# A hybrid trunk layer on one core: one PSUM pool, blocks kept in SBUF at a hand-over, a staggered output pass, and earlier weight loads

## The chip, the cores and the metric

The kernel runs on one core of a Trainium2 chip, as one program. The metric is the device time of one execution in microseconds; lower is better. A core has five engines that run their own instruction queues: TensorE (PE in the profile; its weight loads are PEld), VectorE (DVE), ScalarE (ACT), GpSimd (POOL) and SyncE (SP), which issues nearly all transfers here. TensorE writes to PSUM, which has eight banks of 128 x 512 float32.

## The reference

One layer over 2048 tokens of width 1024, all in float32:

```
h  = rmsnorm(x) ; proj = h @ w_in                        # 1024 -> 5648 columns
y_a = u_b * conv3(u_c * u_h)                             # short convolution mixer, 1024 wide
y_b = rmsnorm_grouped(ssd_scan(silu(conv4(xbc)), dt) * silu(z))   # Mamba-2 mixer, 1024 wide
x  = x + concat(y_a, y_b) @ w_out                        # 2048 -> 1024
x  = x + square(relu(rmsnorm(x) @ w_up)) @ w_down        # 1024 -> 4096 -> 1024
out = rmsnorm(x)
```

## The kernel before

**Arithmetic.** Every float32 operand is split into a rounded high part and a remainder (`hi`, `lo`: a cast on ScalarE, a subtraction on VectorE), and a product is three matmuls, hi x hi, hi x lo and lo x hi. The large projections use the seven-product scheme of Strassen and Winograd on 2 x 2 blocks: tokens in two blocks of 512, contraction in halves, two column tiles of 128. The seven operands of the token side are called b11, t1, t2, b21, t3, b22, t4. They lie in `places`: place 0 holds b11 and t1, place 1 t2 and b21, place 2 t3 and b22, place 3 t4, each four times, for k = 0 to 3, as tiles uh and ul of four buffers per place.

**Stages.** The input projection runs in two halves of 1024 tokens (`first_half`, 20 pairs of column tiles; `second_half`, 22). The scan's first half runs beside the second. `Output` then does the output projection in four passes of 16 units; a unit is one block of 512 tokens times one tile of 128 output columns, 24 matmuls into one PSUM bank, an addition of the residual on VectorE (L1452) and a store. Pass 0 and 1 take the contraction's first half, pass 2 and 3 the second; passes 0 and 2 take token blocks 0 and 1, passes 1 and 3 blocks 2 and 3. In a pass the two blocks alternate for every column tile d. The scan's second half runs beside units 0 to 44. The MLP follows in two halves of 16 pairs, then the down projection and its rest.

**A pair.** `chain` runs the seven products, 12 matmuls each, with accumulators x, y (PSUM tag mm) and w (tag mw); w is seeded with a copy of x after b11, except in the first two pairs of the MLP (`fresh`). After each product come the eviction, then work on the next pair's weights, then `after(name)`. The generator `ahead` first issues the next pair's loads (`next(ahead)`, into `wraw`, three buffers) after the product t1; its four splits are taken after b21 (two), b22 and t4. In the later halves the sums of weights come back from DRAM (`sums_d`), with three loads at the start and a fourth in between.

**Preparation of the other half.** `prepare` is a generator of 32 steps (22 where the sums of squares are there already). It loads two token blocks, sums squares, forms the inverse root, loads the blocks again (tiles nb), scales them (L393), subtracts them into the seven operands (L208) and stores those in DRAM (`stored`: hm_d or hn_d). `after` takes one step at each product. At the last pair of a half, `refresh` fetches the operands of the next half place by place (tiles rb; `fetch`) and splits them (`settle`, L344 and L345).

**The hand-over.** For the MLP's first half, `prepare(0, ...)` runs during the last output pass: `hook` is called twice in a unit, at half of it and at its end, and takes one or two steps. The operands go to hn_d and are fetched again: place 2 at call 19 of the pass, place 3 at 22, place 0 at 28 and place 1 at 31, each settled when it has come and its uh and ul buffers are free; block 2's operands of the output projection occupy the buffers of place 0, block 3's those of place 1. The MLP's first weights are loaded before unit 62; two splits are taken there, one before unit 63, one after it.

**PSUM.** The pool `ps` (tag tp, two banks) lives throughout. Pool `pa` has six banks up to the end of the output projection (mm three, mw one, yo and yd of the scan one each); it is closed, and `pw` opened in its place (mm four, mw two).

**Order.** The source calls the engines in the order described, but each engine's instruction order is made by the compiler from the dependences and its own estimate; neighbours can change places. Each engine then takes its queue in order.

Of the kernel before, what the change touches and what calls it, by code (L numbers as in the profile page):

```python
# [11 lines left out]
F32 = mybir.dt.float32  # L12
# [27 lines left out]
def trunk(ctx: ExitStack, tc: tile.TileContext, x, w_in, w_dt, w_out, w_up, w_down, cvec, hrow, out):  # L40
# [9 lines left out]
    accs = {}  # L50

    edge = ctx.enter_context(tc.tile_pool(name="edge", bufs=1, side="right")).tile([P, 24], F32, name="edge")
    nc.gpsimd.memset(edge, 0.0)
# [61 lines left out]
        nc.tensor.matmul(out, wlo, hi, start=False, stop=(k == nk - 1))  # L115

    def psum(tag, name, bufs=1):
        pool = ps if tag == "tp" else accs["pool"]
        return pool.tile([P, 512], F32, tag=tag, name=name, bufs=bufs)

    class Rstd:

# [67 lines left out]
    class Seven:  # L190
# [53 lines left out]
        def chain(self, groups, ws, ahead, evict, after):  # L244

            n = sum(len(g) for g in groups)
            pm = [{} for _ in groups]
            got = []
            seeds = self.seeds = set()
            bank = lambda acc: psum(*(("mw", "pw", accs["mw"]) if acc == "w" else ("mm", "p" + acc, accs["mm"])))  # L250
            fresh = max(accs.get("fresh", 0), 0)
            accs["fresh"] = fresh - len(groups)
            PRODUCTS = (
                ("b11", 0, 0, "x"),
                ("t1", 1, 0, "y"),
                ("t2", 1, 1, "x"),
                ("b21", 0, 1, "w"),
                ("t3", 2, 0, "x"),
                ("b22", 2, 1, "y"),
                ("t4", 3, 0, "x"),  # L260
            )
            for name, wn, half, acc in PRODUCTS:
                at = half * n
                for gi, g in enumerate(groups):
                    seeded = acc in pm[gi]
                    if not seeded:
                        pm[gi][acc] = bank(acc)
                    p = pm[gi][acc]
                    i, j = WHERE[name]
                    for k, place in enumerate(g):  # L270
                        hi, lo = (t[:, (at + k) * P : (at + k + 1) * P] for t in ws[wn])
                        h = [t[:, j] for t in place[i]]
                        kw = dict(skip_group_check=seeded)
                        nc.tensor.matmul(p, hi, h[0], start=not seeded and k == 0, stop=False, **kw)  # L274
                        nc.tensor.matmul(p, hi, h[1], start=False, stop=False, **kw)  # L275
                        nc.tensor.matmul(p, lo, h[0], start=False, stop=(k == len(g) - 1), **kw)  # L276
                    at += len(g)
                for gi in range(len(groups)):
                    if name == "b11" and gi >= fresh:
                        pm[gi]["w"] = bank("w")  # L280
                        nc.scalar.copy(pm[gi]["w"], pm[gi]["x"])  # L281
                        seeds.add(gi)
                    evict(name, gi, pm[gi])
                if ahead is not None:
                    if name == "t1":
                        next(ahead)
                    got += take(ahead, {"b21": 2, "b22": 1, "t4": 1}.get(name, 0))
                after(name)
            return got
# [51 lines left out]
        def settle(self, places, i, got):  # L341
            for p, t in zip(places, got):
                p[i] = self.place(i)
                nc.scalar.copy(p[i][0], t)  # L344
                nc.vector.tensor_tensor(out=p[i][1], in0=t, in1=p[i][0].bitcast(F32), op=ALU.subtract)  # L345

# [8 lines left out]
        def prepare(self, h, src, base, accs=None):  # L355
# [26 lines left out]
                st.whole(rs[bb])  # L382
                yield
            for k in range(4):
                ts = [self.raw("nb") for _ in range(4)]
                b11, t1, t2, b21, t3, b22, t4, b12 = (t[:, i] for t in ts for i in range(2))
                blocks = ((b11, 0, k), (b12, 1, k), (b22, 1, 4 + k), (b21, 0, 4 + k))
                for o, bb, f in blocks:
                    nc.sync.dma_start(o, src[h * NBB + bb][:, f])
                yield  # L390
                yield
                for o, bb, f in blocks:
                    nc.vector.scalar_tensor_tensor(  # L393
                        out=o, in0=o, scalar=col(base, f), in1=rs[bb], op0=ALU.mult, op1=ALU.mult
                    )
# [5 lines left out]
                for i in range(3):  # L401
                    nc.sync.dma_start(self.stored[h][k][:, 2 * i : 2 * i + 2], ts[i])
                nc.sync.dma_start(self.stored[h][k][:, 6], t4)
                yield

        def facc(self):
            return self.up.tile([P, TB], F32, tag="facc", name="facc", bufs=2)
# [10 lines left out]
    class Proj(Seven):  # L418
# [105 lines left out]

        def group(self, bb, ws, tiles, work, tag="mm"):

            pm = [psum(tag, "pm", accs[tag]) for _ in tiles]
# [255 lines left out]
        def first_half(self, ws):  # L783
            self.last_sums()
            late = self.prepare(1, x, C_NMIX)
            for m, what in enumerate(self.PAIRS):
# [7 lines left out]
                    ahead = self.weights(0, self.PAIRS[m + 1])  # L794

                def after(name):
                    next(late, None)
                    if last:
                        self.refresh(name)

# [21 lines left out]

    class Mlp(Seven):
        stored = hn_d

        def tmp(self, name):
            return self.up.tile([P, TB], F32, tag="utmp", name=name, bufs=8)
# [61 lines left out]
        def half(self, h, ws, late):  # L889
            for q in range(NQ):  # L890
# [10 lines left out]
                    self.new = [{} for _ in range(4)]  # L901

                def after(name):
                    next(late, None)
                    if not last:
                        return
                    if h == 0:
# [125 lines left out]
        def rest(self, ws):  # L1033
# [12 lines left out]
            for bb, t0, w in ((0, 0, TB), (1, 0, TB // 2), (1, TB // 2, TB // 2)):  # L1046
# [13 lines left out]
                for (d, fs, blocks), (whi, wlo) in ws:  # L1060
                    for i in range(2):
# [1 line left out]
                        if not at:  # L1063
                            continue
                        step()
                        pm = psum("mm", "pm", 4)[:, 0:w]
# [90 lines left out]
    class Scan:  # L1157
# [96 lines left out]
        def back(self, n):  # L1254
# [6 lines left out]
            yo = psum("yo", "yo")  # L1261
# [4 lines left out]
            yd = psum("yd", "yd")  # L1266
# [25 lines left out]
            pss = psum("tp", "pss", 2) if self.bufs == 1 else psum("mw", "pss", accs["mw"])  # L1292
# [73 lines left out]
    class Output:  # L1366
# [1 line left out]


        PASSES = [(0, ((0, 0), (1, 1))), (0, ((2, 2), (3, 0))), (1, ((0, 1), (1, 2))), (1, ((2, 0), (3, 1)))]  # L1370
        UNITS = [(i, b, d) for i, bs in PASSES for d in range(KD) for b, _ in bs]
        WEIGHTS = [(i, d) for i, _ in PASSES for d in range(KD)]

        def __init__(self, places):
# [64 lines left out]
        def unit(self, n, hook):  # L1439

            i, b, d = self.UNITS[n]
            self.residual(n + 1)
            if n % 2 == 0:
                self.weights(n // 2 + 2)
            pm = psum("mm", "pm", accs["mm"])
            whi, wlo = self.ws[n // 2]
            for k in range(KD):
                if k == KD // 2:
                    hook(2 * n)
# [8 lines left out]
        def square(self, b, d, t):  # L1458
# [2 lines left out]
                self.accs.append(self.xp.tile([P, TB], F32, tag="facc", name="facc", bufs=2))  # L1461
                nc.scalar.activation(self.accs[b], t, AF.Square)
            else:
                sq = psum("mw", "sq", accs["mw"])
# [21 lines left out]
            put(1, 3, 1, 90, (94, 94, 95, 95))  # L1486


    accs.update(mm=3, mw=1)
    c4 = ctx.enter_context(ExitStack())  # L1490
    with ExitStack() as c1:
        accs["pool"] = c1.enter_context(tc.tile_pool(name="pa", bufs=1, space=PS, reuse_waits="tile"))
        proj = Proj()
        with ExitStack() as c2:
            proj.open(c2, 0)
# [33 lines left out]
        mlp.raws = c4.enter_context(tc.tile_pool(name="ur", bufs=1, side="right", reuse_waits="tile"))  # L1529
        mlp.up = proj_out.xp  # L1530
        mlp.us = c4.enter_context(tc.tile_pool(name="us", bufs=1, side="right", reuse_waits="tile"))
        late = mlp.prepare(0, x1_d, C_NMLP, proj_out.accs)
# [90 lines left out]
```

## Time and profile before

| what | value |
|---|---|
| median of 3 runs | 2684.56 us (2682.47 to 2686.77) |
| profiled execution, its own time | 2686.92 us |
| its span, first to last instruction | 2685.2 us |
| TensorE, VectorE, ScalarE, GpSimd busy | 2608.8, 1876.7, 1431.9, 147.9 us |
| mean granted TensorE clock | 0.992 of full |
| moved by DMA | 551.64 MB, mean 205 GB/s |

Times in the profile count from the first instruction. A timeline row gives the start, the duration, the engine, the source line, the operation and its tiles; in brackets stands the idle time of the engine just before it and what ended that. A row of a view by stretches gives the stretch, its length, the busy time and number of instructions of PE, PEld, DVE, ACT and POOL, then the granted clock, the share of the DMA engines' time and GB/s. A row of grouped instructions ends in busy us, mean ns of one, and the idle time before them. A row of transfers ends in their number, the size of one and the us from issue to landing. SPq, ACTq and the like are the engines' issuing queues. Matmuls are pipelined: the duration in a row overlaps the next, and the distance of starts is what counts.

### The profile page before, as it was taken

The page shows a single profiled execution, that of the slowest core. Times are in us where ns is not written, and L with a number is a line of the kernel's source. Part 1 is how long each engine was busy: PE and PEld are TensorE (multiplying, and loading weights), DVE is VectorE, ACT ScalarE, POOL GpSimd, SP SyncE. Part 2 cuts the span into 40 slices and gives each one's busy share as a digit, 9 for nine tenths or more (in the row PEclk, how much of TensorE's full clock was granted, in tenths as well). Part 3 has the DMA queues.
Part 4 walks back from the last instruction along what each step waited for, and adds up shares of the span by engine and source line. Part 5 has one row for each costly group of instructions (what it writes and reads, how often), then busy time and mean ns, then how long its engine had stood idle before and what let it go on. Part 6 is the DMA issues. An engine that isn't in the chain of part 4 may idle for free. (4 is left out here: it accounts for less than half of the span.)

```text
span 2685.2 us, 33606 instructions
## 1 busy us (share of the span) xinstructions
PE 2608.8 (97%) x12024; PEld 2126.4 (79%) x12024; DVE 1876.7 (70%) x2524; ACT 1431.9 (53%) x2176; POOL 147.9 (6%) x162
## 2 busy tenths in 40 slices
PE   7999999999999999998989999999999999999998
PEld 5778888788887888776877788888887888888887
DVE  7996667667667676666668655644447877888985
ACT  6644345766667676666326455655555444444443
POOL 0010000111111101111000000000000000000001
PEclk9999999999999999999999999999999999999999
DMA  3585345645545588876598875765558545665762
GB/s 144 194 312 185 130 141 203 183 152 180 178 153 171 161 278 259 252 209 210 196 311 292 328 255 192 253 238 203 184 207 276 168 152 152 199 223 169 243 207 74
DMA packets 297479, 551.64 MB, mean 205 GB/s; under 512 B 26720, under 2 KB 142432, under 8 KB 297312
## 3 DMA queue, kind: packets, MB, share of 16 engines
q1 hardware_dynamic: 297312, 549.50, 61.6%
q8 instruction: 94, 1.54, 0.2%
q14 instruction: 73, 0.60, 0.1%
HBM read 362.23 MB, written 187.17 MB: 205 GB/s over the span
## 5 line engine op out<-in xcount | busy, mean ns | idle before, releaser
L274 PE MATMUL px<-uh,whi 128*128 128x512 f32 x1672 | 660.3, 395 | 23.3 <-DVE xt L1452 7.7
L276 PE MATMUL px<-uh,wlo 128*128 128x512 f32 x1672 | 653.7, 391 | 2.2 <-DVE wlo L101 2.2
L275 PE MATMUL px<-ul,whi 128*128 128x512 f32 x1672 | 654.2, 391 | 0.6 <-DVE ul L345 0.5
L274 PEld LDWEIGHTS px<-uh,whi 128*128 128x128 f32 x1672 | 315.4, 189 | 101.1 <-issue 9.5
L101 DVE TENSOR_TENSOR wlo<-wraw,whi 128x1024 fp32r<-128x1024 f32 x214 | 223.7, 1045 | 227.5 <-ACT whi L100 221.7
L276 PEld LDWEIGHTS px<-uh,wlo 128*128 128x128 f32 x1672 | 315.4, 189 | 70.4 <-DVE wlo L101 3.8
L275 PEld LDWEIGHTS px<-ul,whi 128*128 128x128 f32 x1672 | 315.7, 189 | 65.5 <-DVE ul L345 1.8
L100 ACT CAST whi<-wraw 128x1024 fp32r<-128x1024 f32 x214 | 193.5, 905 | 316.1 <-PE px L275 205.6
L274 PE MATMUL py<-uh,whi 128*128 128x512 f32 x836 | 327.8, 392 | 4.7 <-DVE acc L994 3.5
L100 ACT CAST whi<-s 128x1024 fp32r<-128x1024 f32 x210 | 219.4, 1046 | 210.5 <-PE py L275 74.1
L275 PE MATMUL py<-ul,whi 128*128 128x512 f32 x836 | 326.1, 390 | 0.0
L276 PE MATMUL py<-uh,wlo 128*128 128x512 f32 x836 | 325.9, 390 | 0.0
L101 DVE TENSOR_TENSOR wlo<-s,whi 128x1024 fp32r<-128x1024 f32 x210 | 255.3, 1217 | 72.6 <-ACT whi L100 69.6
L113 PE MATMUL pm<-uh,whi 128*128 128x512 f32 (+1 forms) x648 | 252.2, 390 | 2.1 <-ACT uh L204 2.1
L114 PE MATMUL pm<-ul,whi 128*128 128x512 f32 (+1 forms) x648 | 249.3, 385 | 0.0
L115 PE MATMUL pm<-uh,wlo 128*128 128x512 f32 (+1 forms) x648 | 249.0, 384 | 0.0
L274 PEld LDWEIGHTS py<-uh,whi 128*128 128x128 f32 x836 | 157.5, 188 | 39.3 <-DVE acc L994 3.9
L276 PEld LDWEIGHTS py<-uh,wlo 128*128 128x128 f32 x836 | 157.2, 188 | 33.1 <-DVE wlo L101 0.2
L275 PEld LDWEIGHTS py<-ul,whi 128*128 128x128 f32 x836 | 157.3, 188 | 32.2
L274 PE MATMUL pw<-uh,whi 128*128 128x512 f32 x418 | 163.6, 391 | 1.4 <-ACT pw L281 1.4
L276 PE MATMUL pw<-uh,wlo 128*128 128x512 f32 x418 | 162.7, 389 | 0.0
L275 PE MATMUL pw<-ul,whi 128*128 128x512 f32 x418 | 162.7, 389 | 0.0
(220 smaller groups left out, 3719.0 us busy)
## 6 DMA issues: line engine op xcount, KB each, us to landing
hid_d<-e SPq DMA_DIRECT2D x96, 512.0 KB, 4.2
rh<-hid_d SPq DMA_DIRECT2D x96, 512.0 KB, 4.4
wraw<-w_in SPq DMA_DIRECT2D x68, 512.0 KB, 3.9
wraw<-w_down SPq DMA_DIRECT2D x104, 256.0 KB, 3.7
wraw<-w_up SPq DMA_DIRECT2D x48, 512.0 KB, 4.7
dec<-rd_d SPq DMA_DIRECT2D x32, 512.0 KB, 5.5
wraw<-w_out SPq DMA_DIRECT2D x32, 512.0 KB, 5.6
x_d<-xt SPq DMA_DIRECT2D x64, 256.0 KB, 3.7
```

What stands on the lines that cost most here:

```text
L100: nc.scalar.copy(hi, raw)
L101: eng.tensor_tensor(out=lo, in0=raw, in1=hi.bitcast(F32), op=ALU.subtract)
L113: nc.tensor.matmul(out, whi, hi, start=(k == 0), stop=False)
L114: nc.tensor.matmul(out, whi, lo, start=False, stop=False)
L115: nc.tensor.matmul(out, wlo, hi, start=False, stop=(k == nk - 1))
L274: nc.tensor.matmul(p, hi, h[0], start=not seeded and k == 0, stop=False, **kw)
L275: nc.tensor.matmul(p, hi, h[1], start=False, stop=False, **kw)
L276: nc.tensor.matmul(p, lo, h[0], start=False, stop=(k == len(g) - 1), **kw)
```

## The change

1. `psum` knows one pool. Six banks are tags k0 to k5. Up to the end of the output projection mm goes round k0, k1, k2 and mw is k3, with k4 and k5 for the scan's yo and yd; after it mm goes round k0, k1, k2, k4 and mw round k3, k5.
2. In `chain` the next pair's loads are issued after b11, not after t1.
3. `after` takes a step of the preparation at two products of seven in `first_half`, at three of seven in the MLP's first half.
4. The last output pass runs block 3 one column tile behind block 2 (its units: block 2 tile 0, block 2 tile 1, block 3 tile 0, block 2 tile 2, ...), so that block 2 ends with unit 61.
5. For the MLP's first half nothing goes to hn_d. The tiles of place 0 lie in the output projection's ry buffers, those of place 1 in a new pool `stay` (three buffers; the fourth is a raw buffer); those of places 2 and 3 are split at once, in `stow`. Place 0 is settled at the end of unit 61, place 1 after unit 63.
6. `hook` takes one step at each call. The MLP's first weights are loaded before unit 60, with a split before each of the units 61, 62 and 63 and one after.

```diff
+    turns = {"mm": itertools.cycle(("k0", "k1", "k2")), "mw": itertools.cycle(("k3",))}
     def psum(tag, name, bufs=1):
-        pool = ps if tag == "tp" else accs["pool"]
-        return pool.tile([P, 512], F32, tag=tag, name=name, bufs=bufs)
+        if tag in turns:
+            tag = next(turns[tag])
+        return ps.tile([P, 512], F32, tag=tag, name=name, bufs=bufs)
...
                 if ahead is not None:
-                    if name == "t1":
+                    if name == "b11":
                         next(ahead)
...
         def settle(self, places, i, got):
             for p, t in zip(places, got):
                 p[i] = self.place(i)
+                t = t[:, 0:1] if i == 3 else t
...
-                ts = [self.raw("nb") for _ in range(4)]
+                ts = self.blocks(h, k)
...
+                self.stow(h, k, ts)
+                yield
+
+        def stow(self, h, k, ts):
+            for i in range(3):
+                nc.sync.dma_start(self.stored[h][k][:, 2 * i : 2 * i + 2], ts[i])
+            nc.sync.dma_start(self.stored[h][k][:, 6], ts[3][:, 0])
...
 (first_half)
                 def after(name):
-                    next(late, None)
+                    if name in ("b11", "b21"):
+                        next(late, None)
...
 (Mlp)
+        def blocks(self, h, k):
+            if h:
+                return super().blocks(h, k)
+            return [self.early(), self.stay(k), self.raw("nb"), self.raw("nb")]
+
+        def stow(self, h, k, ts):
+            if h:
+                return super().stow(h, k, ts)
+            self.held.append(ts[0:2])
+            for i in (2, 3):
+                self.settle(self.places[k : k + 1], i, ts[i : i + 1])
...
                 def after(name):
-                    next(late, None)
+                    if name in ("b11", "t2", "t3"):
+                        next(late, None)
...
 (Output)
-        UNITS = [(i, b, d) for i, bs in PASSES for d in range(KD) for b, _ in bs]
+        UNITS = [(i, b, d) for i, bs in PASSES[:3] for d in range(KD) for b, _ in bs]
+        UNITS += [(1, b, d - b + 2) for d in range(KD + 1) for b in (2, 3) if 0 <= d - b + 2 < KD]
...
+        mlp.held = []
+        mlp.early = lambda: proj_out.raw("first")
+        mlp.stay = lambda k: mlp.raw("nb") if k == 3 else stay.tile([P, 2, TB], F32, tag="stay", name="stay", bufs=3)
         late = mlp.prepare(0, x1_d, C_NMLP, proj_out.accs)
 
-        held = {}
-        fetches, settles = {19: 2, 22: 3, 28: 0, 31: 1}, {21: 2, 24: 3, 30: 0}
-
         def hook(at):
-            u = at - 2 * 48
-            for _ in range(1 + (u % 3 == 0)):
-                next(late, None)
-            if u in settles:
-                i = settles[u]
-                mlp.settle(mlp.places, i, held[i])
-            if u in fetches:
-                i = fetches[u]
-                held[i] = mlp.fetch(0, i)
+            next(late, None)
+            if at == 2 * 61 + 1:
+                mlp.settle(mlp.places, 0, [t[0] for t in mlp.held])
 
         for n in range(48, 64):
-            if n == 62:
+            if n == 60:
                 ahead = mlp.sums_of(0, 0)
                 next(ahead)
-                ws = take(ahead, 2)
-            elif n == 63:
-                ws += take(ahead, 1)
+            elif n > 60:
+                ws = take(ahead, 1) if n == 61 else ws + take(ahead, 1)
             proj_out.unit(n, hook)
+        mlp.settle(mlp.places, 1, [t[1] for t in mlp.held])
         ws += take(ahead)
-        mlp.settle(mlp.places, 1, held[1])
-    accs.update(mm=4, mw=2, fresh=2, pool=c4.enter_context(tc.tile_pool(name="pw", bufs=1, space=PS, reuse_waits="tile")))
+        c7.close()
+    turns.update(mm=itertools.cycle(("k0", "k1", "k2", "k4")), mw=itertools.cycle(("k3", "k5")), fresh=("k3", "k5"))
```

More of the change, by code (lines that the diff above doesn't have):

```diff
@@ L249, in chain @@
             seeds = self.seeds = set()
-            bank = lambda acc: psum(*(("mw", "pw", accs["mw"]) if acc == "w" else ("mm", "p" + acc, accs["mm"])))
-            fresh = max(accs.get("fresh", 0), 0)
-            accs["fresh"] = fresh - len(groups)
+            bank = lambda acc: psum("mw" if acc == "w" else "mm", "p" + acc)
+            fresh = turns.pop("fresh", ())
+            if fresh:
+                turns["fresh"] = fresh[1:]
             PRODUCTS = (
@@ L278, in chain @@
                 for gi in range(len(groups)):
-                    if name == "b11" and gi >= fresh:
+                    if name == "b11" and not fresh:
                         pm[gi]["w"] = bank("w")
@@ L400, in prepare @@
                 self.sub(t4, b21, t2)
-                for i in range(3):
-                    nc.sync.dma_start(self.stored[h][k][:, 2 * i : 2 * i + 2], ts[i])
-                nc.sync.dma_start(self.stored[h][k][:, 6], t4)
+                self.stow(h, k, ts)
                 yield
+        def blocks(self, h, k):
+            return [self.raw("nb") for _ in range(4)]
+        def stow(self, h, k, ts):
+            for i in range(3):
+                nc.sync.dma_start(self.stored[h][k][:, 2 * i : 2 * i + 2], ts[i])
+            nc.sync.dma_start(self.stored[h][k][:, 6], ts[3][:, 0])
         def facc(self):
@@ L525, in group @@
         def group(self, bb, ws, tiles, work, tag="mm"):
-            pm = [psum(tag, "pm", accs[tag]) for _ in tiles]
+            pm = [psum(tag, "pm") for _ in tiles]
             for k in range(KD):
@@ L824, in trunk, with blocks @@
         stored = hn_d
+        stay = None
+        def blocks(self, h, k):
+            if h:
[7 more added lines that the diff above has]
+                self.settle(self.places[k : k + 1], i, ts[i : i + 1])
         def tmp(self, name):
@@ L1065, in rest @@
                         step()
-                        pm = psum("mm", "pm", 4)[:, 0:w]
+                        pm = psum("mm", "pm")[:, 0:w]
                         todo = [(b * len(fs) + k, j, f) for b, j in at for k, f in enumerate(fs)]
@@ L1260, in back @@
             state = self.state[g]
-            yo = psum("yo", "yo")
+            yo = psum("k4", "yo")
             for j in range(4):
@@ L1265, in back @@
             nc.tensor.matmul(st, t["btok"], t["xde"], start=True, stop=True)
-            yd = psum("yd", "yd")
+            yd = psum("k5", "yd")
             for i in range(HG):
@@ L1291, in back @@
             yield
-            pss = psum("tp", "pss", 2) if self.bufs == 1 else psum("mw", "pss", accs["mw"])
+            pss = psum("tp", "pss", 2) if self.bufs == 1 else psum("mw", "pss")
             nc.tensor.matmul(pss[:, 0:L], ones, ssq, start=True, stop=True)
@@ L1442, in unit @@
             self.residual(n + 1)
[L1443 to L1446, printed above, removed]
+            m = (2 * i + b // 2) * KD + d
+            if b % 2 == 0:
+                self.weights(m + 2)
+            pm = psum("mm", "pm")
+            whi, wlo = self.ws[m]
             for k in range(KD):
@@ L1463, in square @@
             else:
-                sq = psum("mw", "sq", accs["mw"])
+                sq = psum("mw", "sq")
                 nc.scalar.activation(sq, t, AF.Square)
@@ L1486, in schedule @@
             put(1, 3, 1, 90, (94, 94, 95, 95))
-    accs.update(mm=3, mw=1)
     c4 = ctx.enter_context(ExitStack())
     with ExitStack() as c1:
-        accs["pool"] = c1.enter_context(tc.tile_pool(name="pa", bufs=1, space=PS, reuse_waits="tile"))
         proj = Proj()
```

3 lines of the change are left out of this document (2 added, 1 removed).

## The prediction

> **What bounds the kernel now.** I read the page's totals first, then the busy time in stretches of 50 us, then every wait of TensorE in order of time, and for the long waits the queues of VectorE, ScalarE and SyncE around them. The totals say that TensorE is the bound nearly everywhere:
>
> ```profile
> PE 2608.8 (97%) x12024; PEld 2126.4 (79%) x12024; DVE 1876.7 (70%) x2524; ACT 1431.9 (53%) x2176; POOL 147.9 (6%) x162
> ```
>
> So a gain can only come from the stretches where TensorE is not full. By stretch (TensorE busy and matmuls first; then weight loads, DVE, ACT, POOL; granted clock, DMA share, GB/s):
>
> ```profile
> 150.00:200.00 50.00, 47.12 (x204) 37.53 (x202) 49.20 (x64) 23.68 (x29) 7.63 (x9) 1.00 0.86 320
> 1350.00:1400.00 50.00, 50.00 (x222) 41.42 (x221) 27.17 (x36) 8.80 (x10) 0.00 (x0) 1.00 0.91 311
> 1400.00:1450.00 50.00, 38.14 (x147) 28.60 (x147) 38.58 (x46) 30.13 (x40) 0.00 (x0) 0.86 0.81 277
> 1450.00:1500.00 50.00, 49.82 (x220) 40.93 (x219) 46.42 (x64) 30.30 (x45) 0.00 (x0) 1.00 0.91 330
> 1500.00:1550.00 50.00, 44.11 (x183) 35.46 (x182) 31.19 (x45) 20.85 (x31) 0.00 (x0) 0.93 0.87 327
> 2050.00:2100.00 50.00, 44.92 (x183) 35.79 (x182) 38.05 (x56) 15.63 (x21) 0.00 (x0) 0.93 0.74 248
> 1200.00:1250.00 50.00, 39.72 (x199) 31.81 (x198) 31.73 (x49) 39.79 (x80) 7.55 (x6) 0.93 0.77 234
> ```
>
> A full stretch holds 222 matmuls of 512 columns, so one costs 50/222 = 0.225 us, and missing matmuls turn into time: a count takes in the stall, its restart and any slow clock. In the stretch of the hand-over from the output projection to the MLP (1400 to 1450) 75 are missing, 16.9 us; at 1500 to 1550, in the MLP's first half, 39, 8.8 us; at 150 to 200, in the first half of the input projection, 18, 4.1 us. The two last rows are losses of like size in places that the change hardly touches (the scan beside the output projection, and the start of the down projection). The waits behind these counts, from the timeline of TensorE:
>
> ```profile
> 174.78 0.50 PE L276 MATMUL px<-uh,wlo 128*128 128x512 f32 x1 [1.49 <-DVE wlo L101]
> 1220.30 0.33 PE L1231 MATMUL ptb<-ident,bc 128*128 128x128 f32 x1 [2.91 <-DVE state L1279]
> 1408.78 0.77 PE L274 MATMUL px<-uh,whi 128*128 128x512 f32 x1 [7.67 <-DVE xt L1452]
> 1431.94 0.50 PE L274 MATMUL px<-uh,whi 128*128 128x512 f32 x1 [2.05 <-DVE e L851]
> 1520.27 0.80 PE L274 MATMUL px<-uh,whi 128*128 128x512 f32 x1 [5.51 <-ACT whi L100]
> ```
>
> A long wait costs more than itself. In short windows that begin at such a restart the clock is low:
>
> ```profile
> 1220.00:1224.00 4.00, 3.70 (x18) 3.14 (x19) 3.46 (x5) 3.06 (x5) 2.81 (x2) 1.00 0.88 214
> 1408.00:1417.00 9.00, 7.66 (x17) 5.01 (x18) 3.60 (x5) 3.42 (x4) 0.00 (x0) 0.52 1.00 354
> 1520.00:1527.00 7.00, 6.36 (x16) 4.58 (x17) 7.00 (x11) 3.33 (x5) 0.00 (x0) 0.58 0.77 308
> ```
>
> After 2.91 us idle the granted clock stayed at 1.00; after 7.67 and 5.51 us it was 0.52 and 0.58. From the restart to the window's end, 8.22 us held 17 matmuls where 3.8 us would do, and 6.73 us held 16 where 3.6 would: 4.4 and 3.1 us, in which the small waits inside are counted.
>
> **The change part by part.**
>
> **The hand-over (1400).** TensorE ends the last output unit at about 1401 and waits 7.67 us for that unit's own eviction. VectorE and ScalarE show why:
>
> ```profile
> 1403.40 2.36 DVE L101 TENSOR_TENSOR wlo<-s,whi 128x1024 fp32r<-128x1024 f32 x2 [0.46 <-ACT whi L100]
> 1405.68 2.35 DVE L345 TENSOR_TENSOR ul<-rb,uh 128x1024 fp32r<-128x1024 f32 x2
> 1407.95 0.68 DVE L1452 TENSOR_TENSOR xt<-pm,xt 128x512 f32<-128x512 f32 x1
> 1410.32 1.04 ACT L344 CAST uh<-rb 128x1024 fp32r<-128x1024 f32 x1 [3.59 <-DMA rb<-hn_d]
> ```
>
> The eviction (xt, L1452) stands in VectorE's queue behind two weight splits and two settles of blocks; the next settle then waits for blocks that went out to DRAM and come back (rb from hn_d). The DMA view of 1300 to 1450 gives that round trip:
>
> ```profile
> hn_d<-nb SPq DMA_DIRECT2D x12, 512.0 KB, 3.6
> rb<-hn_d SPq DMA_DIRECT2D x12, 512.0 KB, 7.2
> hn_d<-nb SPq DMA_DIRECT2D x4, 256.0 KB, 3.5
> rb<-hn_d SPq DMA_DIRECT2D x4, 256.0 KB, 3.5
> ```
>
> The change removes all 32 of these transfers, 2 x 7 MiB of about 41 MB in that window, and the waits for them. The casts and subtractions of the settles stay in number (16 each); those of places 2 and 3 move forward, to the end of each block's `stow`, where TensorE is full and DVE has 23 us free in 50 (row 1350).
>
> The token blocks a unit apart set free the operands of block 2 after unit 61 instead of 62, so place 0 is settled during units 62 and 63, 2 x 24 x 0.2265 = 10.9 us. What VectorE must do there, by the spacing of the rows above (1.15 each for a 1024-wide operation, 0.6 for a 512-wide one): four settles 4.6, the combination and split of two weight sums 2 x (1.2 + 1.15) = 4.7, one eviction 0.6; together 9.9 of 10.9 us. The last eviction is then on time, within about a microsecond. The wait for it stays: by the code 90 matmul banks are taken before unit 0, so unit 63 has bank k0, and the MLP's first product starts at k0 again, in one pool as in two. Its price is now one eviction with its latencies, about 1 us (bounds: 0.7, the operation alone, and 7.67, today's wait). Place 1 has the products b11 and t1 as cover, 24 matmuls or 5.4 us, for four settles of 4.6 us; only the first is needed at that point. In the first MLP pair VectorE has about 4.6 us of settles beside its usual work, so I leave another 2 us for late evictions such as the 2.05 us at 1431. The hand-over goes from 16.9 to 3 us: **-13.9**, with bounds of -5 (a stall of 5.51 with its 3.1 of slow clock and 3 of small waits stays) and -16.9.
>
> **The preparation thinned out (150 and 1500).** `prepare` has 32 steps. Run at each of 7 products it takes 4.6 pairs; at 3 of 7 (MLP) 10.7 of 16 pairs; at 2 of 7 (input projection) 16 of 20. In both places it is done before the last pair fetches what it stored, so nothing spills there. Its work on VectorE, from the groups of 1400 to 1525:
>
> ```profile
> L393 DVE SCALAR_TENSOR_TENSOR nb<-nb,cv,facc 128x512 f32<-128x512 f32 x16 | 11.4, 747 | 1.2 <-DMA nb<-x_d 1.2
> L208 DVE TENSOR_TENSOR nb<-nb 128x512 f32<-128x512 f32 x16 | 10.6, 687 | 0.1
> L377 DVE TENSOR_TENSOR facc<-facc,lx 128x512 f32<-128x512 f32 x12 | 8.3, 689 | 3.1 <-ACT lx L372 2.9
> L171 DVE RECIPROCAL facc<-facc 128x512 f32<-128x512 f32 x2 | 6.7, 3350 | 0.2 <-ACT facc L170 0.2
> ```
>
> That is 37 us. A pair lasts 84 x 0.225 = 18.9 us and needs of VectorE about 12 to 13 without it (splits, sums, three additions, by the spacings above). Over 4.6 pairs the preparation adds 8 a pair, some 20 of 18.9: over-full, as the stretches 150 (49.2 of 50) and 1450 (46.4) show. Over 10.7 pairs it adds 3.5, over 16 pairs 2.3: 16 and 15 of 18.9. So the deficits go, less some 0.5 us each: **-8.3** (bounds 0 and -8.8) and **-3.5** (bounds 0 and -4.1).
>
> What it costs: for 11 and 16 pairs instead of 5 VectorE is at 80 to 85%, in a queue that runs in order, and a bunched step (four operations of 0.75, or a reciprocal of 3.35 us) can make an eviction late. The nearest rows are waits such as the 1.49 us at 174.78; I take **+1.5** in all, bounds 0 and +6 (about one such wait in every fourth of the 22 pairs that newly carry the work).
>
> **Weight loads at the first product.** The stall at 1520 has this shape on SyncE and ScalarE:
>
> ```profile
> 1509.12 2.94 SPq L389 DMA_DIRECT2D nb<-x_d  x4
> 1512.10 0.91 SPq L95 DMA_DIRECT2D wraw<-w_up  x2
> 1519.17 1.04 ACT L100 CAST whi<-wraw 128x1024 fp32r<-128x1024 f32 x1 [3.12 <-DMA wraw<-w_up]
> ```
>
> The weight loads stood behind four block loads of the preparation in the one queue and came 7 us later, when ScalarE already waited. Put ahead of `after("b11")` they pass those, and have three products to land (8.1 us) instead of two. That secures the 8.8 us a second time; it is not counted twice. In steady pairs TensorE waits for no weights, so elsewhere I price the earlier load at 0. What hides it is the third weight buffer; where that is not yet free, SyncE stands still at the load:
>
> ```profile
> SPq L95 <- DVE wlo L101: 251.7, 87, 11.1
> SPq L302 <- DVE wlo L101: 106.5, 26, 6.0
> ```
>
> That is 2.9 us on average for the first kind. Stores, scan loads and accumulator loads queued behind can be a product later (2.7 us): bounds 0 and +4 over the start of the down projection and the scan, value 0.
>
> **One pool.** The same eight banks with the same turns (three, then four, for x and y; one, then two, for w); the unseeded first two pairs stay two. Price 0; bounds -1 and +1. The instruction order on each engine is made anew from the changed source, which can move waits such as that before 1245, 7.37 us: bounds -3 and +3 for all of this, value 0.
>
> Sum: -13.9 - 8.3 - 3.5 + 1.5 = -24.2 us. The profiled execution took 2686.92 us (span 2685.2), 2.4 above the median 2684.56; set against the median, 2684.56 - 24.2 = 2660.4 us.
>
> On the clock: the Trainium skill, page "TensorE: Matmul & The Clock Gate", Part 1 on the HAM clock gate, says that the array falls to half rate after about 3.4 us without work and needs about 3.4 us of work to come back. The rows agree on the threshold (2.91 us free of cost, 5.51 not), but not on the way back: full rate came later, so a relapse costs 3.1 to 4.4 us here, where by the page I would estimate 1.7. By the page's figure the first rival below would come out at 2665.
>
> **The rivals.**
> *1. VectorE or ScalarE is late at the hand-over after all.* The reckoning leaves 1 us of 10.9 free on VectorE, and the split of the third weight part waits for a slot that unit 62 frees. If the eviction of unit 63 comes over 3.4 us late, the clock falls too: 5.51 + 3.1 instead of 3 left, plus 5.6 us: 2666. With today's full wait and clock, 7.67 + 4.4: 2669.5. For it: the order in the 1403 to 1408 rows. Against: DMA waits, which delayed those splits, fall away.
> *2. The MLP's first half stays short.* VectorE in the first pairs carries the settles, the sums of squares and two reciprocals; if the deficit only moves, the 8.3 are missing: 2668.7. For it: 46.4 of 50 at 1450. Against: the rate of steps is under half. With rival 1 it makes 2675.
> *3. Slower: SyncE blocks.* If a weight load that waits for its buffer holds up the scan's and the hidden layer's transfers by a product, TensorE waits in every pair. There are 20 + 22 + 16 + 16 = 74 pairs; 24.2/74 = 0.33 us a pair eats the gain, and 0.5 gives 2684.6 + 37 - 24 = 2697. For it: the 87 waits at L95. Against: the load is delayed by the same buffer today, and in the steady stretches TensorE misses nothing.
> *4. Nothing of it shows*, because the stalls reappear one stage later: 2684.
>
> **How the numbers follow.** My forecast (2653 to 2666): 0.62. Rival 1: 0.15; rival 2: 0.12; both: 0.04; rival 3: 0.04; rival 4: 0.03. Two tenths of a per cent, 5.4 us, is about what can be told from no change (the three runs span 2682.47 to 2686.77). Forecast and rivals 1, 2 and both lie more than that below: faster 0.93; same 0.03; slower 0.04. The range takes the forecast's low end, less a little for a reordering in its favour (2652), up to both rivals nearly (2673).
>
> **What would show it.** Right: no transfers of hn_d between 1300 and 1400; a wait under 3 us at the first px of the MLP with the clock at 1.00; over 218 matmuls in each 50 us after it; 220 at 150 to 200 with DVE near 42; blocks prepared (L393) until about the eleventh MLP pair and the sixteenth of the projection. Wrong: a wait over 3.4 us and a clock near 0.5 at the hand-over, an ended preparation that leaves evictions late in the pairs, or new waits in the scan's stages or at the start of the down projection.

## The result: 2660.05 us, and the profile after

| | before | changed |
|---|---|---|
| median | 2683.51 us of 4 runs (2682.35 to 2686.77) | 2660.05 us of 4 runs (2658.11 to 2665.81) |
| ratio | | 0.9916, 95% interval 0.9902 to 0.9931 |
| profiled execution, its own time (span) | 2686.92 (2685.2) | 2658.11 (2656.4) us |

The time forecast was 2660.4 us, in a range from 2652 to 2673. No run of one kernel overlaps those of the other. The page's first line of the changed kernel, and its stretches of 50 us as shown for before:

```profile
PE 2602.2 (98%) x12024; PEld 2124.8 (80%) x12024; DVE 1874.3 (71%) x2524; ACT 1436.5 (54%) x2178; POOL 146.1 (6%) x162
```

```profile
150.00:200.00 50.00, 50.00 (x222) 41.41 (x221) 42.15 (x45) 26.59 (x32) 8.24 (x9) 1.00 0.43 158
1200.00:1250.00 50.00, 41.72 (x204) 33.30 (x203) 32.46 (x51) 40.65 (x81) 6.62 (x5) 0.90 0.81 238
1350.00:1400.00 50.00, 50.00 (x223) 41.35 (x221) 33.03 (x42) 18.20 (x19) 0.00 (x0) 1.00 0.61 204
1400.00:1450.00 50.00, 49.12 (x217) 40.21 (x216) 38.74 (x53) 30.88 (x46) 0.00 (x0) 1.00 0.67 236
1450.00:1500.00 50.00, 50.00 (x222) 41.44 (x221) 32.71 (x43) 28.33 (x43) 0.00 (x0) 1.00 0.54 194
1500.00:1550.00 50.00, 50.00 (x222) 41.28 (x221) 37.80 (x50) 25.44 (x39) 0.00 (x0) 1.00 0.93 334
2000.00:2050.00 50.00, 44.38 (x184) 34.89 (x183) 38.60 (x52) 23.98 (x35) 0.00 (x0) 0.97 0.90 308
2050.00:2100.00 50.00, 48.79 (x215) 40.11 (x215) 43.26 (x57) 22.36 (x26) 0.00 (x0) 1.00 0.54 164
```

The stretches at 150 and 1500 are full, 18 and 39 matmuls more than before, and the hand-over misses 5 instead of 75. Together 127 matmuls of 0.225 us, 28.6 us; the two profiled executions differ by 28.8 us in their own times. The medians differ by less, 23.5 us: the profiled execution of before lay 3.4 us above its median, that of the changed kernel is the fastest of its four runs, 1.9 us below. A second profile of before, below, has fewer matmuls missing. The stretch at 1200 keeps its loss. The start of the down projection, now across 2050, misses 45 matmuls in the stretches 2000 and 2050 together, where it missed 43 (before had 218 in the first of them).

The hand-over in the changed kernel, first TensorE, then VectorE:

```profile
1398.82 0.39 PE L115 MATMUL pm<-uh,wlo 128*128 128x512 f32 x1
1399.05 0.39 PE L276 MATMUL py<-uh,whi 128*128 128x512 f32 x1
...
1400.18 0.49 PE L276 MATMUL px<-uh,whi 128*128 128x512 f32 x1
...
1425.36 0.50 PE L276 MATMUL px<-uh,whi 128*128 128x512 f32 x1 [0.88 <-ACT s L871]
```

```profile
1398.29 1.22 DVE L348 TENSOR_TENSOR ul<-stay,uh 128x1024 fp32r<-128x1024 f32 x1 [1.07 <-ACT uh L347]
1399.43 0.68 DVE L1478 TENSOR_TENSOR xt<-pm,xt 128x512 f32<-128x512 f32 x1
```

The last eviction ends about a microsecond after the last output matmul, as reckoned, but TensorE does not stand still for it: the compiler put the first five matmuls of t1 (py, in a bank long free) ahead of b11 (px, in the bank of unit 63). The next wait is 0.88 us, 26 us later.

The preparation lasts longer. These are the issues of its stores in the changed kernel, with first and last start:

```profile
L412 SPq DMA_DIRECT2D hm_d<-nb x12: 319/348/584, 238.8 to 312.5; - x12
L412 SPq DMA_DIRECT2D hn_d<-nb x12: 319/374/1128, 1505.2 to 1584.8; - x12
```

Only the preparation of the MLP's second half still stores to hn_d, from 1505 on; nothing of it is left between 1300 and 1400. By the count of px, py and pw matmuls up to the last stores (313 and 1586), at 28 of one line a pair, the preparation took 12.3 pairs of the projection and 9.7 of the MLP.

### The profile page after: what moved, and what is told of

Its sections match the earlier page's. It is cut to its first block, busy times and chain, and to the rows that moved or that the text cites. A ratio compares the mean times of both kernels' runs of the same rounds, so it can differ in the third digit from the quotient of the medians.

```text
span 2656.4 us, 33528 instructions
## 1 busy us (share of the span) xinstructions
PE 2602.2 (98%) x12024; PEld 2124.8 (80%) x12024; DVE 1874.3 (71%) x2524; ACT 1436.5 (54%) x2178; POOL 146.1 (6%) x162
## 4 chain that ended last, share of the span: by engine, by line
PE 59%; issue 26%; ACT 5%; DMA 4%; DVE 4%; POOL 1%; SPq 0%; POOLq 0%; DVEq 0%; ACTq 0%
PE px L276 9%; PE px L277 9%; PE px L278 9%; PE py L276 4%; PE py L277 4%; PE py L278 4%; PE pm L113 4%; PE pm L114 4%; PE pm L115 3%; PE pw L276 2%; PE pw L277 2%; PE pw L278 2%; ACT whi L100 1%; ACT dec L1267 1%; DMA dec<-rd_d 1%
## 5 line engine op out<-in xcount | busy, mean ns | idle before, releaser
L347 ACT CAST uh<-rh 128x1024 fp32r<-128x1024 f32 (+1 forms) x128 | 120.3, 943 | 80.4 <-PE py L278 62.4
```

## The experiments

e1 to e4 ran in the same rounds on one chip, as did e5 to e8 on a second and e9 to e12 on a third (e12 is one execution, for its profile). The ratios are to the kernel before in the same rounds; "gain" is 1 minus the ratio, times 2684 us.

| kernel | ratio | 95% interval | gain |
|---|---|---|---|
| changed kernel, first measurement | 0.9916 | 0.9902 to 0.9931 | 22.5 us |
| e1, two pools | 0.9916 | 0.9902 to 0.9931 | 22.5 |
| e2, round trip | 0.9958 | 0.9944 to 0.9973 | 11.3 |
| e3, no stagger | 0.9911 | 0.9897 to 0.9925 | 23.9 |
| e4, full preparation | 0.9964 | 0.9953 to 0.9976 | 9.7 |
| e5, before, only thinned | 0.9941 | 0.9923 to 0.9960 | 15.8 |
| e6, before, only early loads | 0.9976 | 0.9964 to 0.9988 | 6.4 |
| e7, loads at t1 | 0.9924 | 0.9910 to 0.9938 | 20.4 |
| e8, pss in tp | 0.9902 | 0.9887 to 0.9918 | 26.3 |
| e9, changed kernel again | 0.9911 | 0.9896 to 0.9927 | 23.9 |
| e10, pss in tp late | 0.9895 | 0.9880 to 0.9910 | 28.2 |
| e11, pss in tp again | 0.9905 | 0.9889 to 0.9920 | 25.5 |

**e1: the changed kernel with two pools.**

```diff
-        return ps.tile([P, 512], F32, tag=tag, name=name, bufs=bufs)
+        pool = turns["pool"] if tag[0] == "k" else ps     # "pa", and a new "pw" after the output projection
+        return pool.tile([P, 512], F32, tag=tag, name=name, bufs=bufs)
...
```

> The changed kernel with the two PSUM pools of before (a new pool opened after the output projection). Theory P (the prediction: one pool is worth nothing, the last eviction costs about 1 us either way): 2660 to 2662 us, first px of the MLP 1 to 2 us after the last pm, and no more matmuls missing at 1400 to 1450 than in the changed kernel (5). Rival Q (the single pool lets the compiler put t1's product, in a bank long free, ahead of b11's, and so hides the eviction; with two pools TensorE waits for it): one wait of 1 to 3 us at the first px, behind xt, 1 to 3 us slower than the changed kernel, 5 to 15 more matmuls missing there.

The first px, the last eviction and ScalarE's casts with two pools:

```profile
1402.15 0.47 PE L277 MATMUL px<-uh,whi 128*128 128x512 f32 x1 [1.06 <-ACT uh L348]
...
1401.32 0.68 DVE L1479 TENSOR_TENSOR xt<-pm,xt 128x512 f32<-128x512 f32 x1
...
1399.09 2.95 ACT L348 CAST uh<-stay 128x1024 fp32r<-128x1024 f32 x3 [2.57 <-PE pm L115]
```

Q is right about the order: here b11 stays first and TensorE waits 1.06 us. The eviction ends at 1402.00. The profile names a cast instead, which ends at 1402.04, so the trace does not separate the two; but the cast's tiles (stay) belong to place 1, and b11 reads place 0 alone, so by the code it is the eviction. P is right about the price: one matmul more is missing at 1400 to 1450 than in the changed kernel (6 for 5), and the times don't resolve it. The single pool is worth about a microsecond at most.

**e2: the changed kernel, but place by place through DRAM.**

```diff
-            if h:
-                return super().stow(h, k, ts)
+            return super().stow(h, k, ts)              # blocks() likewise
...
+        fetches, settles = {19: 2, 22: 3, 25: 0, 31: 1}, {21: 2, 24: 3, 27: 0}   # hook as before; place 0 at 25, not 28
```

> The changed kernel, but the MLP's first blocks go to DRAM and come back as before (places 2, 3, 0, 1 fetched at calls 19, 22, 25, 31 of the last output pass, two steps at every third call); stagger, one pool, thinned preparation and loads at the first product stay. Theory P (the blocks that stay in SBUF carry the hand-over's gain, since place 1 can only be fetched when a raw buffer is free and then takes 7 us to land): 6 to 13 us slower than the changed kernel, 25 to 60 matmuls missing at 1400 to 1450, ACT waiting for rb. Rival R (the stagger alone gives the time, the transfers were hidden): under 3 us slower, under 15 missing.

TensorE and ScalarE at the hand-over, and the stretches:

```profile
1402.22 0.49 PE L276 MATMUL py<-uh,whi 128*128 128x512 f32 x1 [1.60 <-ACT uh L347]
1403.67 0.79 PE L277 MATMUL py<-ul,whi 128*128 128x512 f32 x1 [0.95 <-DVE ul L348]
1405.94 0.80 PE L277 MATMUL py<-ul,whi 128*128 128x512 f32 x1 [0.62 <-DVE ul L348]
1414.87 0.50 PE L276 MATMUL pw<-uh,whi 128*128 128x512 f32 x1 [1.84 <-ACT uh L347]
```

```profile
1413.77 1.04 ACT L347 CAST uh<-rb 128x1024 fp32r<-128x1024 f32 x1 [7.30 <-DMA rb<-hn_d]
```

```profile
1400.00:1404.00 4.00, 1.45 (x5) 0.71 (x4) 4.00 (x6) 3.83 (x5) 0.00 (x0) 0.90 1.03 400
1404.00:1408.00 4.00, 3.38 (x8) 2.13 (x8) 4.00 (x4) 2.47 (x4) 0.00 (x0) 0.50 0.75 302
```

```profile
1400.00:1450.00 50.00, 44.69 (x171) 33.94 (x170) 38.35 (x50) 32.21 (x43) 0.00 (x0) 0.90 0.83 306
```

P: 51 matmuls are missing, 46 more than in the changed kernel (10.4 us), ScalarE waits 7.30 us for place 1, and the gain is halved, with the interval clear of the changed kernel's. The 51 are as many as the second profile of before misses there (52, below). So the blocks that stay in SBUF carry the hand-over's gain; the stagger, the one pool and the earlier loading of the MLP's first weights, which e2 keeps, do not bring it without them. No run takes back that earlier loading alone, so its own share is not known. The profiled execution of e2 is the slowest of its six runs, and it misses 18 matmuls at 1500 to 1550 too, after a wait of 2.36 us for VectorE; this has a part in the 11.2 us.

**e3: the changed kernel with the last pass's blocks alternating.**

```diff
-        UNITS += [(1, b, d - b + 2) for d in range(KD + 1) for b in (2, 3) if 0 <= d - b + 2 < KD]
+        # UNITS over all PASSES, as before
-            if at == 2 * 61 + 1:
+            if at == 2 * 62 + 1:
```

> The changed kernel with the last output pass in the order of before (blocks 2 and 3 alternating); place 0 is settled after unit 62 instead of 61. Theory P (VectorE needs about 4.6 us for place 0 and 2.4 for a weight sum in one unit of 5.4, so the last eviction is late by some 2 to 3 us and place 1 after it): 2 to 6 us slower than the changed kernel, 10 to 25 matmuls missing at 1400 to 1450. Rival S (t1 and b11 need place 0 tile by tile, and the queue keeps up): under 1.5 us slower, under 10 missing.

ScalarE and VectorE at the hand-over, and the stretch of TensorE:

```profile
1388.86 3.89 ACT L347 CAST uh<-first 128x1024 fp32r<-128x1024 f32 x4 [2.57 <-PE pm L115]
```

```profile
1391.69 3.49 DVE L348 TENSOR_TENSOR ul<-first,uh 128x1024 fp32r<-128x1024 f32 x3
1395.39 1.23 DVE L348 TENSOR_TENSOR ul<-stay,uh 128x1024 fp32r<-128x1024 f32 x1 [0.22 <-ACT uh L347]
1396.53 0.68 DVE L1477 TENSOR_TENSOR xt<-pm,xt 128x512 f32<-128x512 f32 x1
```

```profile
1400.00:1450.00 50.00, 49.58 (x219) 40.73 (x218) 39.31 (x52) 31.27 (x45) 0.00 (x0) 1.00 0.69 242
```

S: three matmuls are missing and no time is lost. Unit 63 ends at 1396.1, so it begins at about 1390.7 (24 matmuls earlier), but the casts of place 0 begin at 1388.86: its buffers fall free tile by tile, while unit 62 still runs. The subtractions are done by 1395.2, and the last eviction starts at 1396.53. The stagger bought slack that was not needed.

**e4 and e5: the preparation at every product in the changed kernel; thinned alone in the kernel before.** e4 undoes this edit, which is e5's only one:

```diff
                 def after(name):
-                    next(late, None)
+                    if name in ("b11", "b21"):          # Mlp: ("b11", "t2", "t3")
+                        next(late, None)
```

> The changed kernel with one step of the preparation at each of the seven products again, in the projection's first half and the MLP's first half; weight loads stay at the first product. Theory P (VectorE is over-full with eight more us a pair; the earlier loads do not help): 150 to 200 loses about 4 us again and the MLP's first pairs about 9: 9 to 13 us slower than the changed kernel. Rival T (the stall at 1520 was the weights behind the block loads in the one queue; the earlier load cures it, thinning only the first half): 3 to 5 us slower, and 220 matmuls in every 50 us between 1450 and 1550.

> The kernel before, with one edit: the preparation takes a step at two products of seven in the projection's first half and at three of seven in the MLP's first half; loads stay at t1. Theory P (VectorE over-full): 150 to 200 back to 221 or more matmuls and 1500 to 1550 to 218 or more, 9 to 13 us faster than before; the wait of 7 us at the hand-over stays. Rival T (at 1520 the weights in the queue behind the block loads were the cause, and thinning alone leaves them there): 3 to 6 us faster, a wait over 2 us behind whi or wlo stays in the MLP's first half.

Stretches of e4, its longest wait there, then stretches of e5:

```profile
150.00:200.00 50.00, 48.48 (x210) 38.85 (x210) 49.29 (x63) 24.02 (x29) 6.72 (x9) 1.00 0.87 321
1400.00:1450.00 50.00, 47.38 (x207) 38.39 (x206) 41.83 (x54) 31.80 (x46) 0.00 (x0) 1.00 0.64 225
1500.00:1550.00 50.00, 47.25 (x203) 37.12 (x202) 37.33 (x52) 25.69 (x39) 0.00 (x0) 1.00 0.82 310
```

```profile
1515.34 0.51 PE L278 MATMUL px<-uh,wlo 128*128 128x512 f32 x1 [0.94 <-DVE wlo L101]
```

```profile
150.00:200.00 50.00, 50.00 (x223) 41.37 (x222) 42.51 (x45) 26.50 (x32) 8.24 (x9) 1.00 0.43 159
1500.00:1550.00 50.00, 49.16 (x218) 40.40 (x217) 39.85 (x53) 26.34 (x41) 0.00 (x0) 1.00 0.85 308
```

Thinned alone, both places fill up, and 15.8 us are won, above P's 9 to 13, though the interval reaches into it. The two stretches account for 12.2 us of it (54 matmuls more than in the first profile of before); the rest is not traced. The wait at the hand-over, which P expected to stay at 7 us, was 4.66 us. Left out, 13 us are lost. In between stands e4's MLP: VectorE's backlog returns as small waits, 10 matmuls fewer than in the changed kernel at 1400 and 19 at 1500, but no wait at 1500 to 1550 exceeds 0.94 us where before had 5.51. So the long stall needs the late weights too. T is right in this, but not in its time (3 to 5 us) nor in its 220 matmuls.

**e6 and e7: early loads alone; the changed kernel without them.** The edit of e6; e7 makes the reverse one in the changed kernel:

```diff
-                    if name == "t1":
+                    if name == "b11":
                         next(ahead)
```

> The kernel before, with one edit: the next pair's loads are issued after b11 instead of t1. Theory P (a second cure of the 1520 stall, nothing elsewhere): 3 to 9 us faster than before, the wait of 5.5 us behind whi at 1520 gone or under 2 us, 150 to 200 still 15 to 20 matmuls short. Rival U (VectorE's backlog alone made that stall, so an earlier load changes nothing): within 2 us of before, 35 or more missing at 1500 to 1550.

> The changed kernel with the next pair's loads at t1 again. Theory P (nothing in steady pairs, and the thinning has already cured 1520): within 2 us of the changed kernel. Rival V (with blocks prepared over twice as many pairs the loads stand behind block loads more often): 3 to 8 us slower, waits behind whi in the MLP's first half.

e6 in the MLP's first half, the wait and the stretch:

```profile
1507.57 0.50 PE L274 MATMUL px<-uh,whi 128*128 128x512 f32 x1 [2.28 <-ACT whi L100]
```

```profile
1500.00:1550.00 50.00, 44.91 (x191) 34.95 (x190) 33.12 (x45) 25.20 (x37) 0.00 (x0) 1.00 0.87 320
```

Alone the early loads win 6.4 us, as P has it. They shorten the stall to 2.28 us, a little over P's 2, and the granted clock stays at 1.00. But 31 matmuls stay missing: the stretch holds only 8 more than before (1.8 us), so by this profile most of the 6.4 us does not come from this stall, and where it comes from is not shown. On top of the thinning the early loads win 2.1 us against the first measurement of the changed kernel and 3.5 against e9, in different rounds, which the intervals don't resolve. That is over P's 2 and reaches V's 3 to 8; against V, TensorE in e7 has no wait for weights between 1390 and 1990.

**e8, e10, e11: the wait before 1243.** The largest wait of the changed kernel after its start is not the change's work, since before has it too (7.37 us): the scan's norm sum pss waits for bank k3, which it shares with the squares of the third pass. e8 and e11 are one kernel; e10 applies the edit from unit 32 on.

```diff
-            pss = psum("tp", "pss", 2) if self.bufs == 1 else psum("mw", "pss")
+            pss = psum("tp", "pss", 2)
```

> The changed kernel with one edit that no part of the change has: the scan's group norm sum (pss) takes a bank of tag tp during the output projection too, instead of the one bank k3 that it shares with the squares of the last passes (sq). Theory W (the wait of 5.4 us before 1243 is for that shared bank, which VectorE frees late): the wait falls under 3 us and the clock at 1200 to 1250 stays at 1.00, 4 to 8 us faster than the changed kernel. Rival X (the two tp banks are as crowded, or the sum itself is late because ScalarE and VectorE wait for ry): the wait stays over 4 us, within 2 us of the changed kernel.

> The changed kernel, with pss in a tp bank only from unit 32 on, when the squares take k3 (before that in k3, as in the changed kernel). Theory W (only the sharing with the squares hurts): no waits for srstd between 1050 and 1200, the wait before 1243 under 2 us, 4 to 9 us faster than the changed kernel. Rival X (in the squares' pass tp is as crowded): the wait at 1204 to 1220 of 3 us and one at 1243 stay, within 3 us of the changed kernel.

> The kernel of the run with pss in tp throughout, beside the changed kernel in the same rounds. Theory W: 2 to 6 us faster than the changed kernel. Rival X: no difference outside the scatter of 3 us.

The changed kernel, e8 and e10 in turn:

```profile
1243.42 0.80 PE L1317 MATMUL pss<-ssq,ones_r 128*128 128x128 f32 x2 [5.37 <-DVE facc L1492]
```

```profile
1204.14 0.33 PE L1255 MATMUL ptb<-ident,bc 128*128 128x128 f32 x1 [3.48 <-ACT srstd L1319]
```

```profile
1218.35 1.12 PE L1253 MATMUL ptx<-ident,xd 128*128 128x128 f32 x4 [3.12 <-DVE state L1303]
```

The wait is gone in both, and others come up, for ScalarE's srstd (e8) or for the scan's state (e10). By the gains above e8 is 2.4 to 3.8 us ahead of the changed kernel, under W's 4 to 8. Beside each other in the same rounds the changed kernel took 2661.89 us, e10 2655.25 and e11 2656.26, but the intervals overlap, and the three profiled spans are 2653.2, 2653.1 and 2653.3 us. Whether the edit gains anything stays open.

**e9 and e12: both kernels again.**

> The changed kernel unaltered, timed beside the next two. 2657 to 2664 us; no wait over 1.5 us and no lowered clock between 1390 and 1990, as in its first profile.

> The kernel before unaltered, for a second profile. If the wait of 7.7 us at the hand-over and that of 5.5 us at 1520 belong to the kernel, both are there again within 1.5 us. If they depend on how transfers happen to fall in one execution, one of them differs by over 2 us, and the sum of the stretches differs from 29 by as much.

The second profile of before (its own time 2684.47 us), with the two waits and the two stretches:

```profile
1408.61 0.77 PE L274 MATMUL px<-uh,whi 128*128 128x512 f32 x1 [5.34 <-DVE xt L1452]
...
1515.60 0.79 PE L274 MATMUL px<-uh,whi 128*128 128x512 f32 x1 [4.39 <-ACT whi L100]
```

```profile
1400.00:1450.00 50.00, 41.49 (x170) 32.01 (x169) 41.60 (x50) 32.38 (x42) 0.00 (x0) 0.97 0.86 300
1500.00:1550.00 50.00, 44.11 (x180) 35.42 (x179) 29.61 (x42) 21.77 (x32) 0.00 (x0) 0.90 0.84 314
```

The same program missed 52 matmuls at the hand-over in this execution and 75 in the first: 5.2 us, of which 2.3 are the wait itself. So of e12's two cases it is the second: the size of the stall depends on the execution. From this profile the three stretches (52, 42 and, at 150, 19) less the changed kernel's 5 make 108 matmuls, 24.3 us. The changed kernel again (e9) has no wait over 0.70 us between 1390 and 1990, and its granted clock is 1.00 in the stretches from 1400 to 1600.

## Why the prediction was right, by its steps

- **The hand-over, -13.9.** Between the profiles it was 70 matmuls, -15.8; from the second profile of before, 47, -10.6. Mechanism right: e2 gives back 10.4 us there when the blocks go through DRAM. For the 3 us left over for waits, 1.1 were needed.
- **The stagger as its means** failed as a step. "The token blocks a unit apart set free the operands of block 2 after unit 61" is true, but the reckoning that VectorE needs those two units let the settles begin only at a unit's end; they begin earlier, tile by tile, and with one unit they were done in time (e3).
- **One pool, price 0.** Right within 1 us, but not for its reason. "The wait for it stays" was wrong for the changed kernel: the one pool has another instruction order, t1 ahead of b11, which covers the eviction. With two pools the wait of about 1 us is there (e1).
- **The preparation thinned, -8.3 and -3.5, cost +1.5.** The stretches gave -8.8 and -4.1, and no cost is to be seen: the stretches from 200 to 350 hold 220, 223 and 222. Its length was 9.7 and 12.3 pairs where 10.7 and 16 were reckoned from the source, so the steps ran ahead of the products at which the source has them; that the compiler's order does this is the likely reason. In time the edit is worth 13 to 16 us rather than 10.3 (e4, e5), with an interval in e5 that spans 10.7 to 20.7.
- **Early loads, 0 beside the thinning.** 2 us unresolved in the changed kernel, 6.4 us alone. "That secures the 8.8 us a second time" was too much: alone it leaves 31 matmuls missing of 39.
- **The sum.** The forecast of 24.2 us stands to 22.5 and 23.9 us measured. That it fits so closely has luck in it: its terms came from an execution with a long hand-over (16.9 us, the second profile has 11.7), it left more for remaining waits than remained, and it charged a cost of 1.5 that is not to be seen. Taken back one at a time, the blocks in SBUF are worth 11.2 us (e2) and the thinning 12.8 (e4), where the sum had 13.9 and 10.3: the errors lie in opposite directions. The intervals of these runs reach 3 to 4 us to each side, so the shares are rough.
- **The rivals.** 1 and 2 are refuted by the stretches at 1400 and 1500, 3 by full stretches and the unchanged losses of the scan and the down projection, 4 by the time.
- **The clock.** "The rows agree on the threshold (2.91 us free of cost, 5.51 not)" held in that one execution; in the changed kernel's profile the same wait is followed by slow matmuls (last section). From the restart to matmuls at full speed it took 7.9 us in the first profile of before, with small waits inside, and 2.7 in the second. The Trainium skill, page "TensorE: Matmul & The Clock Gate", Part 1, gives about 3.4 us for both the fall and the way back. The runs put values on both sides of the second (2.7 and 7.9 us) and show falls after less idle time than the first (2.88 us, and 1.60 in e2).

## What to carry to other kernels

Background work tied to "one step per product" is a load on VectorE that can be set: divide its total by the time left until it is needed, not by the steps that the loop offers. Data that go to DRAM and come back within one stage are the first thing to look at where a stage ends in a wait for a fetch. And take the size of a stall from two profiled executions before it becomes a term: here it varied by 5 us in a program whose time varied by 2.5.

## What the runs showed of the hardware that was not expected

- One and the same wait sometimes cost the clock and sometimes not. Between two groups of the scan's transposes TensorE idles 2.83 to 2.92 us in eleven of the profiles. In four of them (the first of before, e2, e3, e4) the matmuls after it kept their distance of 0.23 us. In the other seven several came at 0.43 us, in the changed kernel's first profile until 1223.33, as its timeline of TensorE shows (start, duration, and the wait in brackets):

```profile
1219.30 0.33 PE L1255 MATMUL ptb<-ident,bc 128*128 128x128 f32 x1 [2.92 <-DVE state L1303]
...
1220.37 0.63 PE L115 MATMUL pm<-uh,wlo 128*128 128x512 f32 x1
1220.79 0.63 PE L113 MATMUL pm<-uh,whi 128*128 128x512 f32 x1
...
1223.33 0.40 PE L113 MATMUL pm<-uh,whi 128*128 128x512 f32 x1
```

- The transposes on both sides of that wait are short (128 columns). From the last matmul of 512 columns before it to the first after it about 4.0 us pass, in the first profile of before (4.04) as in the changed kernel's (4.05), so this does not tell the two cases apart either. In e7 the first two matmuls of 512 columns after the wait still started 0.32 and 0.23 us before their successors, and the slow ones came behind them: the clock fell after the restart.
- The clock also fell without a long idle time. In e2 TensorE's waits were 1.60, 0.95 and 0.62 us with one to three matmuls between them, and the granted clock was 0.50 from 1404 to 1408. What decides when it falls no run here varied alone, so it stays open.
- The way back does not follow the length of the wait. After 5.34 us (second profile of before) six matmuls ran slowly, after 7.67 us (first profile) fifteen, with small waits among them. After the same wait of 2.9 us for the scan's state it took 2.8 us from the restart in e9 and 6.2 us in e5, with no other wait in between.
